# Retention's prompt outputs placed behind its states, sample columns in a segment of their own

## The chip, the cores and the metric

The kernel runs on one core of one Trainium2 chip. The metric is the device time of one execution in microseconds (us). Before the change the median of three runs is 2833.42 us (2832.51 to 2833.78). A change of about 0.2% is what such a measurement can tell from none.

## The reference

One decoder layer is computed for two groups of tokens that share all weights: a prompt of 256 tokens with 16 learned tokens ahead of it, and 8 single sample tokens that continue from given recurrent states.

```python
x <- LN1(alpha*x + 0.5*SwiGLU_1(x))
x <- LN2(alpha*x + Mixer(x))
x <- LN3(alpha*x + 0.5*SwiGLU_2(x))
```

The mixer projects x (2048 features) to ten parts of 2048 and runs two recurrences side by side: retention (8 heads of 256 x 256 state, a fixed decay gamma per head) and HGRN2 (16 heads of 128 x 128 state, a data-dependent decay per feature). Each is normalised per head, gated, summed and projected back. The part that the change touches is retention:

```python
inner = (q @ k.T) * D                       # D: decay between positions, causal
o     = inner @ v + (q * decay) @ S         # output of a chunk from scores and state
S_new = gamma**C * S + (k * decay).T @ v    # state after the chunk
```

For the prompt, S starts at zero, so all 272 positions can be done with scores alone, and S_new is an output. For each of the 8 sample tokens (C = 1) the given state is updated, S_new = gamma*S + k v, which is an output too; its row of the result is q S_new. Outputs of the program are the new activations of both groups and the four sets of states.

## The kernel before

**Tiling.** Features lie on the 128 partitions, tokens along the free dimension: 280 columns (16 learned, 256 prompt, 8 sample), or 264 where the learned ones are not needed. A weight matrix is streamed in units of eight 128 x 128 blocks (512 KB). For each unit SP issues a load into `raw` (three buffers), ScalarE makes a rounded copy `whi` (L172) and VectorE the remainder `wlo` (L173); both have three buffers. The activations are split in the same way. `dense` (L191) then does three matmuls for each block (L198 to L200): `whi` with the high part, `whi` with the low part, `wlo` with the high part.

**Order.** On TensorE (PE) instructions run in exactly the order in which the program text issues them. On VectorE (DVE), ScalarE (ACT), GpSimd (POOL) and the DMA queues a planner sets the order beforehand: it simulates the engines with its own costs, and at each point gives an engine the ready instruction that comes first in the text (weights are put first). On the chip each engine keeps that order and waits at an instruction whose inputs are late. Tiles with one name or tag share a few buffers, given out in the order of the text; `tmp` (L489) maps some names to rows `d0` to `d15` and others that the first FFN's norm has left free.

**Mixer.** The projections of the mixer are done in eight units (`qkv_groups`, `gate_groups`): for each pair of HGRN2 heads and its retention head, two output chunks each of f, q, i (HGRN2), q, k, v (retention), and one unit later the gates. A group of two chunks is one run of `dense` with 16 turns, two blocks or six matmuls a turn. After each turn `pump` (L532) moves every live *thread* on: `mix_hg` and `mix_ret` are generators, and `yield n` means that the next part is issued n turns later. So the small matmuls of both recurrences lie between the large ones of the projections. `mix_hg` is started 3 turns behind the evacuation of i, 25 turns in the second unit (L580); `mix_ret` 3 turns behind v (L594). The small matmuls take PSUM from four `mx` banks, the projections from four `acc` banks.

**Retention in `mix_ret` (L787).** In order of the text: transposes of v and k with their splits into `vtr` and `ktr` (L794 to L813; the last 16 to 24 rows go to `vtl` and through a row called `sro`); the sample rows of v are written to DRAM (`vrow`, L815); scores `psc` (L820), multiplied with the decay table and split into `sch`, `scl`, `ss3`; states `psr` for both halves of the features (L834 to L844), each copied to `sro` and written out. Then the samples, in two halves of four tokens (L847): `vbr` is loaded, a broadcast of four rows of v to all partitions (512 KB, one buffer); for each half c of the features the states `smr` are loaded (512 KB, three buffers, which `ktr` shares), scaled by gamma on ACT (L855), updated by four DVE instructions (L858) and written out; 12 turns later 16 small matmuls read them (`pqr`, L867) against `qdr`, where each token's q stands in a 32-column slot of its own. The first half's rows are copied to `os` (named `osr` in the profile), the second half's added (L873). `os` is split into `orh` and `orl`. Five turns later follow the outputs `por`, one PSUM bank for each half of the features: columns 0 to 255 from scores and v (L884, L887), columns 256 to 263, the samples, from `orh` and `orl` with a selection matrix (L889), and one copy of all 264 columns to `on` (L890). Head normalisation follows, and then `done_r` marks the unit as ready for its gates (L604).

## Time and profile before

| What | Value |
|---|---|
| Median of the runs | 2833.42 us |
| The profiled execution | 2830.58 us |
| Its span, first to last instruction | 2828.6 us |
| PE busy | 2794.1 us, 99% |
| DVE busy | 1723.7 us, 61% |
| ACT busy | 1370.5 us, 48% |
| DMA | 190 GB/s on average |
| Mixer, from the evacuation of its first group to its last projection | 820 to 1969 us of the span |

All times inside the execution count from the first instruction. The page groups instructions by line, engine, operation and tile (out <- in); a line can be that of a helper. PE is matmuls, PEld weight loads; matmuls overlap in the records, so their ends overlap the next one's start. A wait is the idle time of an engine just before an instruction, put down to what released it. In the views by windows, PEclk is the share of its full clock that TensorE was granted.

### The profile page before, as it was taken

To read this page: it belongs to the slowest core of one execution; us is meant where nothing else is said; L and a number is where in the kernel's file an instruction comes from. 1 tells how busy PE (TensorE), PEld (TensorE's weight loads), DVE (VectorE), ACT (ScalarE), POOL (GpSimd) and SP (SyncE) were. 2 spreads that over 40 slices of the span, in tenths; PEclk is the share of its full clock that TensorE was granted. 3 is DMA by queue.
4 is the path that set the end of the run, shared out by engine and by line. 5 is a ranking of instruction groups with operands and counts; after the bars stand their busy time and mean duration, and the time that the engine had idled before them with its cause. 6 is when DMAs were issued, how large, how long until landed. Compare 5 with 4: busy or idle time off the path is not lost.

```text
span 2828.6 us, 54706 instructions
## 1 busy us (share of the span) xinstructions
PE 2794.1 (99%) x22720; PEld 2759.8 (98%) x22720; DVE 1723.7 (61%) x2821; ACT 1370.5 (48%) x2114; POOL 3.4 (0%) x38
## 2 busy tenths in 40 slices
PE   9999999999999999999999999999999999999999
PEld 9999999999999999999999999999999999999998
DVE  5444444554487777676767776776884444446444
ACT  4444443433354564646565655555554444444333
POOL 0000000000000000000000000000000000000000
PEclk9999999999999999999999999999999999999999
DMA  6555555555557575666665756575555555555654
GB/s 223 172 173 175 174 172 174 172 175 172 174 160 231 175 244 190 216 203 215 198 222 186 240 184 230 180 245 166 180 177 185 184 182 184 183 185 180 180 182 140
DMA packets 155594, 536.29 MB, mean 190 GB/s; under 512 B 17937, under 2 KB 27089, under 8 KB 155345
## 3 DMA queue, kind: packets, MB, share of 16 engines
q1 hardware_dynamic: 155200, 532.65, 59.1%
q8 instruction: 178, 2.92, 0.4%
q14 instruction: 72, 0.58, 0.1%
q10 hardware_dynamic: 144, 0.14, 0.0%
HBM read 502.12 MB, written 30.61 MB: 188 GB/s over the span
## 4 chain that ended last, share of the span: by engine, by line
PE 93%; DVE 2%; DMA 2%; ACT 1%; issue 1%; SPq 0%; ACTq 0%; DVEq 0%
PE up L199 12%; PE up L198 12%; PE up L200 12%; PE dn L199 6%; PE dn L200 6%; PE dn L198 6%; DMA smr<-in_sr 2%; PE pj_v_r L198 1%; PE pj_f L199 1%; PE pj_k_r L198 1%; PE pj_k_r L199 1%; PE pj_v_r L199 1%; PE pj_f L198 1%; PE pj_f L200 1%; PE pj_k_r L200 1%; PE pj_v_r L200 1%
## 5 line engine op out<-in xcount | busy, mean ns | idle before, releaser
L173 DVE TENSOR_TENSOR wlo<-raw,whi 128x1024 fp32r<-128x1024 f32 (+1 forms) x869 | 1062.2, 1222 | 869.3 <-ACT whi L172 862.0
L172 ACT CAST whi<-raw 128x1024 fp32r<-128x1024 f32 (+1 forms) x869 | 909.4, 1046 | 1112.8 <-PE up L199 475.5
L199 PE MATMUL up<-x,whi 128*128 128x280 f32 (+1 forms) x2688 | 773.9, 288 | 0.1
L198 PE MATMUL up<-x,whi 128*128 128x280 f32 (+1 forms) x2688 | 767.5, 286 | 1.1 <-ACT whi L172 1.1
L200 PE MATMUL up<-x,wlo 128*128 128x280 f32 (+1 forms) x2688 | 764.7, 284 | 1.2 <-DVE wlo L173 1.2
L198 PEld LDWEIGHTS up<-x,whi 128*128 128x128 f32 x2688 | 505.8, 188 | 1.9 <-ACT whi L172 1.6
L200 PEld LDWEIGHTS up<-x,wlo 128*128 128x128 f32 x2688 | 505.7, 188 | 1.7 <-DVE wlo L173 1.7
L199 PEld LDWEIGHTS up<-x,whi 128*128 128x128 f32 x2688 | 505.4, 188 | 0.3 <-DVE x L206 0.3
L200 PE MATMUL dn<-h,wlo 128*128 128x280 f32 (+1 forms) x1376 | 395.7, 288 | 0.0
L199 PE MATMUL dn<-h,whi 128*128 128x280 f32 (+1 forms) x1376 | 395.6, 288 | 0.0
L198 PE MATMUL dn<-h,whi 128*128 128x280 f32 (+1 forms) x1376 | 391.9, 285 | 0.0
L198 PEld LDWEIGHTS dn<-h,whi 128*128 128x128 f32 x1376 | 259.1, 188 | 0.1
L199 PEld LDWEIGHTS dn<-h,whi 128*128 128x128 f32 x1376 | 258.4, 188 | 0.1
L200 PEld LDWEIGHTS dn<-h,wlo 128*128 128x128 f32 x1376 | 258.3, 188 | 0.0
L198 PE MATMUL pj_i_h<-x,whi 128*128 128x280 f32 x256 | 75.6, 295 | 6.6 <-DVE q L214 6.2
L198 PE MATMUL pj_g_r<-x,whi 128*128 128x264 f32 x256 | 81.7, 319 | 0.0
L858 DVE SCALAR_TENSOR_TENSOR smr<-vbr,k_r,smr 128x256 f32<-128x256 f32 x128 | 55.2, 479 | 39.1 <-DMA vbr<-vrd 38.2
L199 PE MATMUL pj_i_h<-x,whi 128*128 128x280 f32 x256 | 76.2, 298 | 1.6 <-DVE x L366 1.5
L198 PE MATMUL pj_g_h<-x,whi 128*128 128x264 f32 x256 | 76.0, 297 | 0.0
L200 PE MATMUL pj_i_h<-x,wlo 128*128 128x280 f32 x256 | 75.7, 296 | 0.0
L198 PE MATMUL pj_k_r<-x,whi 128*128 128x280 f32 x256 | 75.1, 293 | 0.0
L198 PE MATMUL pj_v_r<-x,whi 128*128 128x280 f32 x256 | 75.1, 293 | 0.0
(374 smaller groups left out, 5314.2 us busy)
## 6 DMA issues: line engine op xcount, KB each, us to landing
raw<-in_w_up SPq DMA_DIRECT2D x343, 512.0 KB
raw<-in_w_in SPq DMA_DIRECT2D x320, 512.0 KB
raw<-in_w_dn SPq DMA_DIRECT2D x172, 512.0 KB
smr<-in_sr SPq DMA_DIRECT2D x32, 512.0 KB
out_srs<-smr SPq DMA_DIRECT2D x32, 512.0 KB
raw<-in_w_out SPq DMA_DIRECT2D x32, 512.0 KB
smh<-in_sg SPq DMA_DIRECT2D x16, 512.0 KB
out_sgs<-smh SPq DMA_DIRECT2D x16, 512.0 KB
```

Source lines behind the costliest of these rows:

```text
L172: nc.scalar.copy(hi[:, j0:j1, :], raw[:, j0:j1, :])
L173: nc.vector.tensor_tensor(out=lo[:, j0:j1, :], in0=raw[:, j0:j1, :], in1=hi[:, j0:j1, :].bitcast(F32), op=ALU.subtract)
L198: nc.tensor.matmul(o, wh, h, start=k == 0, stop=False)
L199: nc.tensor.matmul(o, wh, l, start=False, stop=False)
L200: nc.tensor.matmul(o, wl, h, start=False, stop=k == nk - 1)
L858: nc.vector.scalar_tensor_tensor(out=sm[:, j, :], in0=vb[:, j, :], scalar=k[:, c, t : t + 1], in1=sm[:, j, :], op0=ALU.mult, op1=ALU.add)
```

## The change

In `mix_ret` the order of the text becomes: transposes; the first half's loads (`vbr` and two `smr`) ahead of the scores; scores; states; then, two turns behind the last state and two turns apart, the two `por` groups with columns 0 to 255 alone and a copy of 256 columns each; two turns later the first half's scaling and updates; 6 turns later its read and copy to `os`, and at once the second half's loads; 10 turns later the second half's updates; 6 turns later its read and the addition; 4 turns later the sample columns, a segment of its own: for each half of the features one plain fp32 matmul of `os` with the selection matrix into a new bank `pos`, and one copy of both to `on`. Head normalisation follows at once. The split of `os` is gone, and with it `orh`, `orl` and the rounded selection matrix `sel_r`.

Two more edits: the small `ktl` gets the name and row `d9`, and `sro`, the copy of the state, alternates between rows `d9` and `d11`; and `mix_hg` starts 8 turns behind i in the first unit instead of 3, and 30 instead of 25 in the second.

```diff
-    sel_r = cst.tile([P, NS], F32R, tag="sel_r", name="sel_r")
...
-    nc.scalar.copy(sel_r, sel)
...
@@ -482,7 +480,7 @@
 
             rows = {n: (r if isinstance(r, list) else [r]) for n, r in {
                 "cos": "d0", "sin": "d1", "gs": ["d2", "d3"], "gt": ["d4", "d5"], "y": "d6", "rot": ["d7", "d8"],
-                "sro": "d9", "osh": "d10", "osr": "d11", "vtl": "d11", "T2": "d12", "T4": "d13", "sqh": "ls1", "sq2": "ls2", "kth": "d14", "hhi": "d14", "hlo": "d15", "pr0": "d14", "pr1": "d15", "pr2": "d10", "rhi": "ls2", "orh": "ls2", "orl": "lnc", "dtab": ["d7", "d8"], "rlo": "lnc",
+                "ktl": "d9", "sro": ["d9", "d11"], "osh": "d10", "osr": "d11", "vtl": "d11", "T2": "d12", "T4": "d13", "sqh": "ls1", "sq2": "ls2", "kth": "d14", "hhi": "d14", "hlo": "d15", "pr0": "d14", "pr1": "d15", "pr2": "d10", "rhi": "ls2", "dtab": ["d7", "d8"], "rlo": "lnc",
                 "sqr": "lnq", "hmean": "lnc", "rv": "rv", "rr": "rr", "rt": "rt",
             }.items()}
 
@@ -577,7 +575,7 @@
                     v = tmp("v", (P, 2, T))
                     nc.scalar.copy(v[:, 0, :], o0)
                     nc.scalar.copy(v[:, 1, :], o1)
-                    start(mix_hg(c0 // 2, st["f"], st["k"], st["q"], v), 25 if c0 == 2 else 3)
+                    start(mix_hg(c0 // 2, st["f"], st["k"], st["q"], v), {0: 8, 2: 30}.get(c0, 3))
                 elif n in ("q_r", "k_r"):
                     sc, w, x0 = (1.0, TL, NMETA) if n == "q_r" else (KSC, T, 0)
                     r = tmp(n, (P, 2, w))
@@ -807,13 +805,42 @@
                         nc.vector.tensor_scalar(out=kh[:, b, c, :], in0=kb, scalar1=d, scalar2=None, op0=ALU.mult)
                         nc.vector.scalar_tensor_tensor(
                             out=kl[:, b, c, :], in0=kb, scalar=d, in1=kh[:, b, c, :].bitcast(F32), op0=ALU.mult, op1=ALU.subtract)
-                    ktl = tmp("sro", (P, P))
+                    ktl = tmp("ktl", (P, P))
                     nc.scalar.activation(ktl[:NB2, :], pt[:NB2, 2 * P : 3 * P], AF.Copy, scale=dec[:NB2, 2, u : u + 1])
                     stack(lambda r: ks3[r, c, :], ktl[:NB2, :], 64)
                     yield 2
                 nc.vector.tensor_copy(qdr[:, :, 0 : NS * 32 : 33], q[:, :, SEQ:])
                 vrow = rows_out(vtl[16:24].rearrange("p c f -> p (c f)"), 256, "vr")
 
+                def load(e):
+                    vb = tmp("vbr", (P, 4, 256))
+                    nc.sync.dma_start(vb, vrow[4 * e : 4 * e + 4, :].partition_broadcast(P))
+                    sms = [tmp("smr", (P, 4, 256), bufs=3) for c in range(2)]
+                    for c, sm in enumerate(sms):
+                        nc.sync.dma_start(sm, A["sr"][u, c, :, 4 * e : 4 * e + 4, :])
+                    return vb, sms
+
+                def update(e, vb, sms):
+                    for c, sm in enumerate(sms):
+                        nc.scalar.mul(sm, sm, GAMMA[u])
+                        for j in range(4):
+                            t = LP + 4 * e + j
+                            nc.vector.scalar_tensor_tensor(
+                                out=sm[:, j, :], in0=vb[:, j, :], scalar=k[:, c, t : t + 1], in1=sm[:, j, :],
+                                op0=ALU.mult, op1=ALU.add)
+                        nc.sync.dma_start(O["srs"][u, c, :, 4 * e : 4 * e + 4, :], sm)
+
+                def read(e, sms):
+                    pq = mx_bank("pqr")
+                    for c in range(2):
+                        for j in range(4):
+                            b = 4 * e + j
+                            nc.tensor.matmul(
+                                pq[32 * j : 32 * j + 32, :256], qdr[:, c, 32 * b : 32 * b + 32], sms[c][:, j, :],
+                                start=c == 0, stop=c == 1, tile_position=(0, 32 * j))
+                    return pq[:, :256]
+
+                first = load(0)
                 psc = mx_bank("psc")
                 for b, (col, l0, n, nk) in enumerate(SCORES):
                     for c in range(2):
@@ -843,38 +870,6 @@
                     nc.sync.dma_start(O["srp"][u, c], so)
                     yield 2
 
-                os = tmp("osr", (P, 256))
-                for e in range(2):
-                    vb = tmp("vbr", (P, 4, 256))
-                    nc.sync.dma_start(vb, vrow[4 * e : 4 * e + 4, :].partition_broadcast(P))
-                    sms = []
-                    for c in range(2):
-                        sm = tmp("smr", (P, 4, 256), bufs=3)
-                        sms.append(sm)
-                        nc.sync.dma_start(sm, A["sr"][u, c, :, 4 * e : 4 * e + 4, :])
-                        nc.scalar.mul(sm, sm, GAMMA[u])
-                        for j in range(4):
-                            t = LP + 4 * e + j
-                            nc.vector.scalar_tensor_tensor(
-                                out=sm[:, j, :], in0=vb[:, j, :], scalar=k[:, c, t : t + 1], in1=sm[:, j, :],
-                                op0=ALU.mult, op1=ALU.add)
-                        nc.sync.dma_start(O["srs"][u, c, :, 4 * e : 4 * e + 4, :], sm)
-                    yield 12
-                    pq = mx_bank("pqr")
-                    for c in range(2):
-                        for j in range(4):
-                            b = 4 * e + j
-                            nc.tensor.matmul(
-                                pq[32 * j : 32 * j + 32, :256], qdr[:, c, 32 * b : 32 * b + 32], sms[c][:, j, :],
-                                start=c == 0, stop=c == 1, tile_position=(0, 32 * j))
-                    if e == 0:
-                        nc.scalar.copy(os, pq[:, :256])
-                    else:
-                        add(os, os, pq[:, :256])
-                hilo = tmp("orh", (P, 256), dt=F32R), tmp("orl", (P, 256), dt=F32R)
-                split(*hilo, os)
-                yield 5
-
                 on = tmp("on_r", (P, 2, TL), bufs=2)
                 on_r[u] = on
                 for c in range(2):
@@ -885,10 +880,22 @@
                                 po[:, l0 : l0 + n], x[:, b, c, :], w[:, col : col + n], start=b + i == 0, stop=False)
                     l0 = SCORES[2][1]
                     nc.tensor.matmul(po[:, l0 : l0 + NMETA], vs3[:, c, :], ss3, start=False, stop=True)
-                    for i, x in enumerate(hilo):
-                        nc.tensor.matmul(po[:, SEQ:TL], x[:, c * P : (c + 1) * P], sel_r, start=i == 0, stop=i == 1)
-                    nc.scalar.copy(on[:, c, :], po[:, :TL])
-                    yield 1
+                    nc.scalar.copy(on[:, c, :SEQ], po[:, :SEQ])
+                    yield 2
+                update(0, *first)
+                yield 6
+                os = tmp("osr", (P, 256))
+                nc.scalar.copy(os, read(0, first[1]))
+                second = load(1)
+                yield 10
+                update(1, *second)
+                yield 6
+                add(os, os, read(1, second[1]))
+                yield 4
+                po = mx_bank("pos")
+                for c in range(2):
+                    nc.tensor.matmul(po[:, c * NS : (c + 1) * NS], os[:, c * P : (c + 1) * P], sel, start=True, stop=True)
+                nc.scalar.copy(on[:, :, SEQ:TL], po[:, : 2 * NS].rearrange("p (c b) -> p c b", c=2))
                 sm_ = tmp("sqr", (P, TL))
                 add(sm_, on[:, 0, :], on[:, 1, :])
                 hilo = tmp("rhi", (P, TL), dt=F32R), tmp("rlo", (P, TL), dt=F32R)
```

## The prediction

> **What bounds the kernel now.** I read the page first, then who TensorE waited for, then the granted clock in windows around those waits, and last the order of single instructions in one unit.

> ```profile
> span 2828.6 us, 54706 instructions
> PE 2794.1 (99%) x22720; PEld 2759.8 (98%) x22720; DVE 1723.7 (61%) x2821; ACT 1370.5 (48%) x2114; POOL 3.4 (0%) x38
> ...
> ```

> TensorE (PE) is the bound. It idles 34.5 us of 2828.6, so any gain must come from that idle time or from time that it spends at a lower clock. The waits of PE name most of the idle time (who waited for whom: total us, times, longest):

> ```profile
> PE por L889 <- ACT orh L205: 8.4, 6, 1.9
> PE pj_i_h L198 <- DVE q L214: 6.2, 1, 6.2
> PE por L889 <- DVE orl L206: 4.6, 6, 0.8
> PE pd L211 <- ACT prodsmh L205: 2.0, 1, 2.0
> ...
> PE pqr L867 <- DVE smr L858: 0.9, 1, 0.9
> PE psr L840 <- DVE vs L529: 0.8, 1, 0.8
> ```

> The two rows on L889 are 13.0 us: in six of eight units the sample matmul inside the retention output waits for the rounded copy `orh` of the sample rows, and then once more for its remainder `orl`. The windows below show a second cost. The first four are the 3.4 us stretches that hold such waits, the others stretches that follow a wait, and the last is ordinary work. After the length come PE busy time and its matmuls; PEclk is the first number after POOL.

> ```profile
> 1172.60:1176.01 3.41, 0.79 (x6) 0.61 (x6) 3.37 (x10) 0.48 (x3) 0.00 (x0) 1.00 0.68 213
> 1612.91:1616.33 3.42, 2.48 (x19) 2.39 (x20) 1.77 (x4) 0.66 (x3) 0.00 (x0) 1.00 0.99 307
> 1752.86:1756.27 3.41, 1.56 (x14) 1.39 (x12) 3.41 (x8) 1.74 (x4) 0.00 (x0) 1.00 0.60 201
> 1899.64:1903.05 3.41, 1.59 (x13) 1.43 (x12) 2.72 (x7) 0.79 (x2) 0.10 (x1) 1.00 0.87 312
> 848.33:851.74 3.41, 3.25 (x14) 3.12 (x14) 3.14 (x10) 0.00 (x0) 0.00 (x0) 0.50 0.31 126
> 920.01:926.84 6.83, 4.17 (x18) 4.17 (x19) 6.80 (x20) 3.96 (x13) 0.00 (x0) 0.50 0.84 285
> 1176.01:1182.83 6.82, 6.82 (x33) 6.82 (x33) 1.11 (x3) 2.71 (x5) 0.00 (x0) 0.50 0.45 139
> 1322.78:1329.61 6.83, 6.83 (x34) 6.83 (x33) 1.23 (x3) 2.89 (x6) 0.00 (x0) 0.50 0.41 121
> 1469.55:1476.38 6.83, 6.83 (x33) 6.83 (x33) 1.11 (x3) 2.71 (x5) 0.00 (x0) 0.50 0.41 138
> 1756.27:1763.10 6.83, 6.29 (x29) 6.30 (x30) 1.95 (x6) 2.45 (x4) 0.00 (x0) 0.50 0.55 180
> 1903.05:1909.87 6.82, 6.82 (x33) 6.82 (x33) 1.69 (x4) 3.80 (x6) 0.00 (x0) 0.50 0.25 84
> 1183.00:1189.83 6.83, 6.83 (x69) 6.49 (x67) 4.35 (x8) 3.73 (x8) 0.00 (x0) 1.00 0.33 98
> ```

> At a granted clock of 0.50, PE does 33 or 34 matmuls in 6.83 us instead of 69, so each such stretch costs half its length, 3.4 us. Five of them (from 1176.01, 1322.78, 1469.55, 1756.27 and 1903.05) begin right behind a stretch with an L889 wait. The stretch at 1612.91, 0.94 us idle, is followed by none; those with 1.82 us idle (1899.64) and more are. So the point from which a wait costs double lies between 0.94 and 1.82 us of idle time in a window of 3.4 us. An L889 wait costs some 2 us of idle time plus 3.4 us of slow clock, and PE still shows as busy in the second part.

> [...]

> **Why L889 waits.** One unit (the third), with PE first, then VectorE (DVE), ScalarE (ACT) and the DMA queue (SP); in brackets the idle time before a row and its releaser:

> ```profile
> 1142.52 0.88 PE L838 MATMUL psr<-vtr,ktr 128*128 128x256 f32 x6
> ...
> 1154.87 1.07 PE L867 MATMUL pqr<-smr,qdr 128*32 128x256 f32 x16
> ...
> 1166.63 1.07 PE L867 MATMUL pqr<-smr,qdr 128*32 128x256 f32 x16
> 1171.35 0.22 PE L750 MATMUL pst<-vm,km 128*128 128x128 f32 x1
> ...
> 1171.82 0.48 PE L884 MATMUL por<-sch,vtr 128*128 128x256 f32 x2
> ...
> 1174.63 0.27 PE L889 MATMUL por<-sel_r,orh 128*128 128x8 f32 x1 [1.86 <-ACT orh L205]
> ```

> ```profile
> 1159.86 0.88 DVE L858 SCALAR_TENSOR_TENSOR smr<-vbr,k_r,smr 128x256 f32<-128x256 f32 x2 [5.63 <-DMA vbr<-vrd]
> ...
> 1164.40 1.67 DVE L858 SCALAR_TENSOR_TENSOR smr<-vbr,k_r,smr 128x256 f32<-128x256 f32 x4
> ...
> 1172.42 1.39 DVE L742 SCALAR_TENSOR_TENSOR smh<-vbh,k,smh 128x128 f32<-128x128 f32 x5
> 1173.73 0.41 DVE L217 TENSOR_TENSOR osr<-osr,pqr 128x256 f32<-128x256 f32 x1
> 1174.06 1.22 DVE L173 TENSOR_TENSOR wlo<-raw,whi 128x1024 fp32r<-128x1024 f32 x1
> 1175.20 0.41 DVE L206 TENSOR_TENSOR orl<-osr,orh 128x256 fp32r<-128x256 f32 x1
> ```

> ```profile
> 1148.59 1.06 ACT L855 ACTIVATE smr<-smr 128x1024 f32<-128x1024 f32 x1 [1.06 <-DMA smr<-in_sr]
> ```

> ```profile
> 1152.41 0.46 SPq L849 DMA_DIRECT2D vbr<-vrd  x1
> ```

> DVE idles 5.63 us for the second broadcast `vbr` (issued at 1152.41, used at 1159.86), is then busy without a break, and reaches the addition of the second half's sample rows only at 1173.73, 6.0 us after `pqr` ended (1166.63 + 1.07). The rounding on ACT, a weight split of 1.22 us and the remainder follow.

> **The change part by part.** A step below is one turn of the projection loop (six matmuls). From the end of the second `pqr` (1167.70) to `pst` (1171.35) are five steps: 0.73 us each.

> *Prompt outputs behind the states, the sample columns alone at the end.* The `por` matmuls move up to 2 and 4 steps behind the last `psr`. Their inputs (scores, `vtr`) are ready there, so no wait goes with them. Both pieces are the same matmuls in another place, 1.1 us each (1171.82 to 1172.8 without the wait): 0. Out go `orh` and `orl`; what comes in is two plain fp32 matmuls of 8 columns on the unrounded rows and one 16-column copy. The nearest fp32 row is the other branch's:

> ```profile
> L774 PE MATMUL po<-sel,osh x32: 175/216/256, 913.2 to 1917.5; 128*128 128x8 f32 x32
> L889 PE MATMUL por<-sel_r,orh x16: 252/273/354, 936.9 to 1903.8; 128*128 128x8 f32 x16
> ```

> It records two for each of its 16 heads, so two matmuls are four records of 0.2 us against four of 0.27 us now: 0, at most 0.2 us a unit either way. ACT and DVE lose 0.4 us a unit each, ACT gains a copy no longer than that; both hide behind PE's 0.73 us steps.

> Does `pos` still wait? Steps from `psr` to the first read go from 14 to 12, with 2.2 us of `por` now in between: read at 1154.87 - 1.5 + 2.2 = 1155.6. Reads go from 12 to 16 steps apart, so the second one stands at 1155.6 + 11.76 (today's distance) + 4 x 0.73 = 1170.3, and `pos`, four steps and `pst` (0.47) on, at 1170.3 + 1.07 + 2.92 + 0.47 = 1174.8. DVE's backlog starts 0.7 us later than today with the first read, so its five `smh` end near 1173.7 + 0.7 = 1174.4 at best, the addition near 1174.8; add 0.45 us from there to PE (1174.14 to 1174.6 for `orh` today): `pos` waits about 0.5 us. Bounds: 0 (the addition is put ahead of the `smh`), and 1.9 (all of DVE's work shifts by the 2.2 us of `por`: 1176.3 + 0.4 against 1174.8). I take 0.6 in six units: 3.6 us lost. Both L889 rows go: 13.0 us gained. At 0.6 us idle, below 0.94, the five slow stretches go too: 5 x 3.4 = 17.1 us gained.

> *Samples loaded ahead, updates listed later.* No transfer is added. The planner already issues well ahead of the text: the L855 of 1148.59 scales a tile whose place in the text is behind the read of 1154.87. So I expect about the same queue orders, and DVE's 5.6 us wait for `vbr` to stay. Behind that wait in DVE's order stand weight splits, and it has been survived by the weights converted ahead. The second read gets 4 steps more: the 0.9 us `pqr` wait goes. `sro` in two buffers takes out ACT's wait for the state write, which has cover anyway: 0.

> ```profile
> ACT sro L842 <- DMA out_srp<-sro: 13.4, 7, 3.4
> ```

> *HGRN2 started 5 steps later in units 0 and 1.* In unit 0 PE waits 2.0 us for `prodsmh`:

> ```profile
> 847.87 0.51 PE L211 MATMUL pd<-prodsmh,ones_r 128*128 128x512 f32 x1 [2.00 <-ACT prodsmh L205]
> ...
> 918.38 1.06 ACT L855 ACTIVATE smr<-smr 128x1024 f32<-128x1024 f32 x1 [3.92 <-DMA smr<-in_sr]
> ...
> 922.67 0.60 PE L198 MATMUL pj_i_h<-x,whi 128*128 128x280 f32 x1 [6.24 <-DVE q L214]
> ```

> Five steps are 3.7 us, more than 2.0, and DVE works off the normalisation in them: 2.0 us and the stretch at 848.33 (3.41 / 2 = 1.7) go, 3.7 us; bounds 0 and 3.7. What is late next in unit 0 is the 6.2 us wait for `q`: ACT stands 3.92 us at the sample load of 918.38, with the evacuation of `q` behind it. That load is still issued behind the first read, so I leave this wait and its slow stretch (920.01, 3.4) where they are; bounds 0 and 9.6 us of gain.

> *Less cover.* DVE and ACT get 5 us less per unit for the same work. DVE is at 61% on the page, and the stretch of slow clock was cover for it. I take 0; bound, by the `psr` row, one wait of 0.8 us a unit: 6 us.

> **Sum.** 13.0 + 17.1 + 0.9 + 3.7 - 3.6 = 31.1 us. The profiled execution took 2830.58 us (span 2828.6 and 2 us around it): 2799.5. The median of the runs is 2.84 us above that execution, so 2802. By the bounds: at best 31.1 + 3.6 + 9.6 = 44.3 less (2789); at worst without new slow stretches 31.1 - 7.5 (rest of the 1.9 us waits) - 3.7 - 6 = 13.9 less (2819). Likeliest range 2793 to 2812.

> **Rivals.**
> *The wait moves to `pos` whole* (18%). DVE's backlog is older than the rounding: the addition itself comes at 1173.73, after PE wanted its result. If it slips by the full 2.2 us, the 8.4 us stay, only the 4.6 go, and two to five slow stretches stay. Gains 4.6 + 0.9 + 3.7 plus 0 to 10.2 us: 2814 to 2824, say 2819. For it: the `smh` row just ahead of the addition. Against it: four steps more between the reads, and no work of ACT and no second wait behind the addition.

> *The `q` wait of unit 0 goes too* (12%): 2802 - 9.6 = 2792, if the later HGRN2 start and the later update move ACT's sample scaling behind the evacuation of `q`. Against: the scaling is ready by the planner's reckoning before `q` ends.

> *The slow stretches stay without the waits* (3%). If the half clock does not come from these waits, only idle time is saved: 2802 + 17.1 = 2819. [...]

> *Slower: the second read waits for the updates* (8%). If ACT and DVE keep to the place in the text, the second half's scaling starts 10 steps behind the first read, near 1165.6; one L855 (1.06), eight L858 (1.67 for four, so 3.3) and two weight splits (2.4) end near 1172.4, 2.1 us after PE wants the read at 1170.3. That is above 1.82, so a slow stretch follows: 5.5 us in each of eight units, 44 us against 34.7 gained: 2843. It decides from about 1 us of waiting on (34.7 / 8 = 4.3 us a unit with the 3.4). Against it: the L855 at 1148.59, which runs ahead of its text.

> *Nothing moves* (7%): the planner's order absorbs the edit, one wait is swapped for others of its size; 2833.

> **How the numbers follow.** My forecast has 52%. From 2789 to 2824 are this case, the `q` case, the moved wait and the stretches that stay: 85%. Within 0.2% (5.7 us, what a measurement of this kernel can tell from no change) is "nothing moves". Faster: 52 + 12 + 18 + 3 = 85%; same 7%; slower 8%.

> **What would show it.** Right: no PE wait for `orh` or `orl`, a wait at the new sample matmul under 0.9 us, no granted clock of 0.50 between 1100 and 1970 us, no wait at `pd`; DVE still idle for `vbr`. Wrong: a wait at `pos` of 1.8 us or more with half clock behind it, a wait at the second sample read, or PE waiting for weights because DVE lost its cover.

## The result and the profile after

The changed kernel takes 2794.25 us in the median of four runs (2792.13 to 2796.78), beside 2832.97 us for the kernel before on the same chip (2829.51 to 2833.78, four runs). The ratio is 0.9866, with a 95% interval from 0.9849 to 0.9883: 38.7 us or 1.3% faster. I had predicted 2802 us, in a range from 2789 to 2824. The profiled execution took 2794.69 us; its span, 2792.6 us, is 36.1 us shorter than the one before.

The page after, its first lines (the span; busy time, share and instructions of each engine):

```profile
span 2792.6 us, 54731 instructions
...
PE 2770.2 (99%) x22720; PEld 2738.7 (98%) x22720; DVE 1723.6 (62%) x2813; ACT 1363.8 (49%) x2111; POOL 3.4 (0%) x38
```

PE has as many matmuls as before, and is busy 23.9 us less (2794.1 - 2770.2): it does the same work faster, for the most part because the clock is higher (0.998 of full speed on average in this execution, 0.991 in the one before; 2.8 us have another source, shown below). Its idle time fell by 12.1 us, from 34.5 to 22.4 (2792.6 - 2770.2). What PE waits for now, in the view of waits (who waited for whom: total us, times, longest):

```profile
PE pst L748 <- DVE km L527: 4.9, 6, 1.2
PE pj_i_h L197 <- DVE q L213: 3.6, 2, 3.2
PE up L197 <- ACT x L204: 2.5, 1, 2.5
PE pj_i_h L198 <- DVE x L365: 1.8, 2, 1.5
```

No row is left for `orh` or `orl`, for `prodsmh` or for the second sample read. Nor is there one for the new sample matmul `pos`. A new row leads instead: in six units the HGRN2 state matmul `pst` waits for `km`, 0.8 us on average. In a second execution of the same kernel that wait is 2.7 us in four units, so its size differs from one execution to the next. (Line numbers of helpers are one lower than before: L197 to L199 are the three matmuls of a block.)

The windows after: 1100 to 1970 us of the span, where the kernel before had five stretches of half clock, and then the one long wait for `q` and the stretch behind it. PEclk is the first number after POOL.

```profile
1100.00:1970.00 870.00, 864.74 (x7331) 845.62 (x7330) 625.73 (x1193) 503.74 (x913) 1.57 (x16) 1.00 0.64 213
914.10:917.51 3.41, 0.86 (x8) 0.66 (x6) 3.41 (x8) 2.57 (x5) 0.00 (x0) 1.00 0.63 202
917.51:924.34 6.83, 5.78 (x24) 5.44 (x25) 3.68 (x10) 2.21 (x8) 0.00 (x0) 0.50 0.97 324
```

Between 1100 and 1970 us PE runs at full clock throughout. The stretch at 917.51 is the only one left inside the mixer in this execution.

The same unit as shown of before (the third), PE and then DVE, in order of time:

```profile
1148.14 1.05 PE L838 MATMUL pqr<-smr,qdr 128*32 128x256 f32 x16
...
1162.58 1.07 PE L838 MATMUL pqr<-smr,qdr 128*32 128x256 f32 x16
...
1166.68 0.30 PE L748 MATMUL pst<-vm,km 128*128 128x128 f32 x1 [0.66 <-DVE km L527]
...
1168.04 0.51 PE L897 MATMUL pos<-sel,osr 128*128 128x8 f32 x4
```

```profile
1145.59 1.22 DVE L172 TENSOR_TENSOR wlo<-raw,whi 128x1024 fp32r<-128x1024 f32 x1
1148.03 1.23 DVE L172 TENSOR_TENSOR wlo<-raw,whi 128x1024 fp32r<-128x1024 f32 x1 [1.22 <-ACT whi L171]
1151.07 1.67 DVE L828 SCALAR_TENSOR_TENSOR smr<-vbr,k_r,smr 128x256 f32<-128x256 f32 x4 [1.82 <-DMA vbr<-vrd]
...
1159.78 0.35 DVE L740 SCALAR_TENSOR_TENSOR smh<-vbh,k,smh 128x128 f32<-128x128 f32 x1
...
1164.66 1.21 DVE L172 TENSOR_TENSOR wlo<-raw,whi 128x1024 fp32r<-128x1024 f32 x1
...
1166.25 0.28 DVE L527 TENSOR_TENSOR km<-ptk,km 16x128 fp32r<-16x128 f32 x1
...
1166.92 0.41 DVE L216 TENSOR_TENSOR osr<-osr,pqr 128x256 f32<-128x256 f32 x1
```

The addition ends at 1167.33, and `pos` starts at 1168.04 without a wait. The last of the `smh` updates now lies at 1159.78, far ahead of the addition; before, five of them stood directly in front of it. What is late is `km`, ready at 1166.53 behind a weight split that begins at 1164.66.

By stages, from the first matmul of a stage to that of the next, in both traces (us):

| Stage | shorter by | my terms for it |
|---|---|---|
| Start and first FFN | -2.5 | 0 |
| First unit, to f of the second (883.68, now 880.99) | 5.2 | 3.7 |
| Second unit, to q_r of the third (1086.79, now 1080.28) | 3.8 | 0.9 |
| Units three to eight, mixer's end, next up projection (to 2560.71, now 2527.45) | 26.8 | 26.5 |
| Last down projection to the end | 2.8 | 0 |
| Sum | 36.1 | 31.1 |

The 26.5 are 13.0 + 17.1 - 3.6; the 0.9 is the wait at the second sample read, which lies in the second unit (at 1023.7 us in the kernel before). The other 2.6 us or so of that unit are the shorter wait for `q`. The first row is the wait of the first up projection for its activations (2.5 us in the row of `up` above), which differs between executions: the first up projection took 528.2 to 531.3 us over all kernels here.

### The profile page after: what moved, and what is told of

It reads as the page before. It is cut to its first block, busy times and chain, and to the rows that moved or that the text cites. A ratio compares the mean times of both kernels' runs of the same rounds, so it can differ in the third digit from the quotient of the medians.

```text
span 2792.6 us, 54731 instructions
## 1 busy us (share of the span) xinstructions
PE 2770.2 (99%) x22720; PEld 2738.7 (98%) x22720; DVE 1723.6 (62%) x2813; ACT 1363.8 (49%) x2111; POOL 3.4 (0%) x38
## 3 DMA queue, kind: packets, MB, share of 16 engines
q8 instruction: 178, 2.92, 0.4%
## 4 chain that ended last, share of the span: by engine, by line
PE 94%; DVE 2%; DMA 2%; ACT 1%; issue 1%; SPq 0%; ACTq 0%; DVEq 0%
PE up L198 12%; PE up L197 12%; PE up L199 12%; PE dn L198 6%; PE dn L197 6%; PE dn L199 6%; PE pj_v_r L197 1%; PE pj_f L198 1%; PE pj_k_r L198 1%; PE pj_v_r L198 1%; PE pj_k_r L197 1%; PE pj_f L199 1%; PE pj_f L197 1%; PE pj_k_r L199 1%; PE pj_v_r L199 1%; PE wo L199 1%
## 5 line engine op out<-in xcount | busy, mean ns | idle before, releaser
L198 PE MATMUL up<-x,whi 128*128 128x280 f32 (+1 forms) x2688 | 774.1, 288 | 0.1
L197 PE MATMUL up<-x,whi 128*128 128x280 f32 (+1 forms) x2688 | 767.5, 286 | 3.8 <-ACT x L204 2.5
L199 PE MATMUL up<-x,wlo 128*128 128x280 f32 (+1 forms) x2688 | 764.8, 285 | 0.8 <-DVE wlo L172 0.7
L197 PEld LDWEIGHTS up<-x,whi 128*128 128x128 f32 x2688 | 505.8, 188 | 4.6 <-ACT x L204 2.8
L199 PEld LDWEIGHTS up<-x,wlo 128*128 128x128 f32 x2688 | 505.9, 188 | 1.2 <-DVE wlo L172 1.2
L198 PEld LDWEIGHTS up<-x,whi 128*128 128x128 f32 x2688 | 505.6, 188 | 0.3 <-DVE x L205 0.3
L198 PE MATMUL dn<-h,whi 128*128 128x280 f32 (+1 forms) x1376 | 395.6, 287 | 0.0
L197 PE MATMUL dn<-h,whi 128*128 128x280 f32 (+1 forms) x1376 | 392.6, 285 | 0.0
L199 PE MATMUL dn<-h,wlo 128*128 128x280 f32 (+1 forms) x1376 | 390.8, 284 | 0.0
L197 PEld LDWEIGHTS dn<-h,whi 128*128 128x128 f32 x1376 | 258.5, 188 | 0.1
L199 PEld LDWEIGHTS dn<-h,wlo 128*128 128x128 f32 x1376 | 258.5, 188 | 0.0
L198 PEld LDWEIGHTS dn<-h,whi 128*128 128x128 f32 x1376 | 258.3, 188 | 0.1
L197 PE MATMUL pj_i_h<-x,whi 128*128 128x280 f32 x256 | 75.2, 294 | 3.9 <-DVE q L213 3.6
L197 PE MATMUL pj_g_r<-x,whi 128*128 128x264 f32 x256 | 79.0, 309 | 0.0
L198 PE MATMUL pj_i_h<-x,whi 128*128 128x280 f32 x256 | 75.5, 295 | 1.9 <-DVE x L365 1.8
L197 PE MATMUL pj_g_h<-x,whi 128*128 128x264 f32 x256 | 75.5, 295 | 0.0
L197 PE MATMUL pj_v_r<-x,whi 128*128 128x280 f32 x256 | 75.0, 293 | 0.0
L197 PE MATMUL pj_k_r<-x,whi 128*128 128x280 f32 x256 | 74.9, 293 | 0.0
L199 PE MATMUL pj_i_h<-x,wlo 128*128 128x280 f32 x256 | 74.9, 293 | 0.0
L198 PE MATMUL pj_v_r<-x,whi 128*128 128x280 f32 x256 | 74.5, 291 | 0.0
```

The lines of the kernel that those rows point to most:

```text
L197: nc.tensor.matmul(o, wh, h, start=k == 0, stop=False)
L198: nc.tensor.matmul(o, wh, l, start=False, stop=False)
L199: nc.tensor.matmul(o, wl, h, start=False, stop=k == nk - 1)
```

## The experiments

Every kernel below computes the whole reference. Times are medians, with the range where there are several runs; a time without a range is a single run; ratios are to the kernel before on the same chip.

**Is it the rounding or the addition that is late?** The kernel before without `orh` and `orl`, everything in its old place:

```diff
-                hilo = tmp("orh", (P, 256), dt=F32R), tmp("orl", (P, 256), dt=F32R)
-                split(*hilo, os)
                 yield 5
...
-                    for i, x in enumerate(hilo):
-                        nc.tensor.matmul(po[:, SEQ:TL], x[:, c * P : (c + 1) * P], sel_r, start=i == 0, stop=i == 1)
+                    nc.tensor.matmul(po[:, SEQ:TL], os[:, c * P : (c + 1) * P], sel, start=True, stop=True)
```

> The kernel before with the rounding of the sample rows alone taken out: columns 256 to 263 come from the unrounded rows in plain fp32, at the same place in the text, five turns behind the second read. Theory A (the addition itself is late, at 1173.73 in the third unit where the matmul is wanted at 1172.77): a wait remains, now for the addition, of about 1.4 us instead of 1.9 + 0.8 in that unit (1174.14 + 0.05 against 1172.77) and 0.3 to 1.4 us in the other five; most stretches at half clock go, since the wait is below 1.8 us; 13.0 - 5 + 5 x 3.4 is up to 25 us gained, with some stretches left 12 to 20. Theory B (the rounding chain on ScalarE and VectorE is the whole cause): no wait at the sample matmul at all, 30 us gained.

Measured: 2815.33 us (2808.07 to 2817.34), ratio 0.9933 (0.9916 to 0.9950). The waits of PE:

```profile
PE por L886 <- DVE osr L217: 5.7, 6, 1.5
```

With neither rounding nor remainder, PE still waits in the same six units, now for the addition itself: 5.7 us of the 13.0. So the addition is late by itself, and the split adds 7.3 us. In the profiled execution one stretch of half clock stays among these six units. It begins at 1460.25 us, behind a wait that leaves 1.45 us idle in its window (3.41 less PE's 1.96):

```profile
1456.84:1460.25 3.41, 1.96 (x19) 1.87 (x17) 3.38 (x10) 0.60 (x3) 0.00 (x0) 1.00 0.67 207
1460.25:1463.66 3.41, 3.41 (x18) 3.41 (x17) 0.98 (x3) 1.96 (x3) 0.00 (x0) 0.50 0.93 294
```

The other five waits leave at most 1.25 us in a window, and no stretch follows them. This execution is the fastest of the four (2808.07 us, mean granted clock 0.997); the other three have 0.995, so they hold more half clock than the trace shows. By the median it is 17.6 us of the gain, without moving anything.

**Is distance alone enough?** The kernel before, with four more turns between the split and the outputs:

```diff
                 split(*hilo, os)
-                yield 5
+                yield 9
```

> The kernel before with nine turns instead of five between the split of the sample rows and the outputs; nothing else. Rival: all that was missing is distance, and the new order of the text is not needed. Four turns are 2.9 us, the waits were at most 1.9 + 0.8: then no wait for orh or orl, no half clock behind the outputs, about 27 to 30 us gained, the 2 us wait of the first unit and its slow stretch left. If the planner fills the time with other work ahead of the addition instead, waits of 1 us or more stay and the gain is under 20 us.

Measured: 2804.64 us (2802.92 to 2807.77), ratio 0.9901 (0.9885 to 0.9918). Waits of PE, and one window row for the same 870 us:

```profile
PE pj_i_h L198 <- DVE q L214: 6.1, 1, 6.1
PE pd L211 <- ACT prodsmh L205: 2.0, 1, 2.0
```

```profile
1100.00:1970.00 870.00, 868.28 (x7355) 848.54 (x7355) 628.10 (x1192) 505.57 (x909) 1.59 (x16) 1.00 0.66 214
```

One number changed gives 28.3 us of the 38.7 (2832.94 - 2804.64): no wait for `orh` or `orl` is left, and these units run at full clock. So most of what the change brings comes from this, that the sample columns come later than their inputs, not that the prompt outputs come earlier. Here `pst` does not wait for `km` either.

**And if the distance is taken back?** The changed kernel with one turn instead of four between the addition and `pos`:

```diff
                 add(os, os, read(1, second[1]))
-                yield 4
+                yield 1
```

> The changed kernel with one turn instead of four between the second read and the sample matmul. The addition of the rows comes 3.3 us behind the end of the second read in the third unit (1163.6 to 1166.9), and the sample matmul is wanted 2.2 us earlier than now: it should wait 2 to 2.5 us there, and 1 to 2.5 us in the units behind. If idle time of 1.8 us or more in a 3.4 us window brings half clock (the threshold read from the trace of before), three or more of these units get a stretch at 0.50 of 3.4 or 6.8 us, and the profiled time rises by 10 to 25 us. If half clock has nothing to do with such waits, only the idle time is added: 6 to 12 us.

Measured: 2821.15 us. The waits, and two pairs of windows (the second pair is the wait of 3.34 us at 1453.78 with what follows it; the first pair holds one of 2.64 us that ends at 1165.70):

```profile
PE pos L897 <- DVE osr L216: 17.4, 6, 3.3
```

```profile
1161.16:1164.57 3.41, 1.90 (x22) 1.11 (x22) 3.38 (x5) 1.91 (x5) 0.00 (x0) 1.00 0.86 350
1164.58:1167.99 3.41, 2.29 (x19) 2.29 (x20) 1.90 (x5) 0.79 (x3) 0.00 (x0) 1.00 0.87 291
1451.30:1454.71 3.41, 0.93 (x8) 0.93 (x8) 2.44 (x6) 0.17 (x1) 0.00 (x0) 1.00 0.74 240
1454.71:1458.12 3.41, 3.41 (x18) 3.41 (x17) 1.15 (x3) 1.60 (x3) 0.00 (x0) 0.50 0.37 148
```

Three turns less cost 27 us against the changed kernel, a little more than the 10 to 25 I expected, since the waits are longer (2.4 to 3.3 us): 17.4 us of waits and four stretches of half clock. The rest of the change is in place here, so without these turns it brings little. The `km` wait is gone here (PE stands at `pos` instead), and one thing I had not expected shows: the wait of 2.64 us is longer than any single L889 wait of before (1.9 us), and no half clock follows it. It lies across a border: 1.51 us of idle time in one window and 1.12 in the next. The borders are counted in steps of 3.41 us from the start of the stretch at 1454.71 (1164.58 lies 85 steps ahead of it); that starts of such stretches lie whole steps apart is read from the trace of before, further down. With 2.48 us idle in one such window half clock follows here, with 1.51 and 1.12 us in two it does not.

**The later HGRN2 start.** The changed kernel with the old start turns, and with `sel_r` left among the constants:

```diff
-                    start(mix_hg(c0 // 2, st["f"], st["k"], st["q"], v), {0: 8, 2: 30}.get(c0, 3))
+                    start(mix_hg(c0 // 2, st["f"], st["k"], st["q"], v), 25 if c0 == 2 else 3)
```

> The changed kernel with HGRN2 started 3 and 25 turns behind i in the first two units, as before, and the unused rounded selection matrix kept, so that all tiles lie as before. The 2.0 us wait at pd comes back, with 1.7 us of half clock: 3.7 us slower than the changed kernel; later units unchanged. If the last down projection takes 251 us again and not 248, its 2.8 us come from where the tiles lie; if 248, from the execution.

Measured: 2799.02 us (2795.46 to 2803.12), ratio 0.9881 (0.9865 to 0.9896).

```profile
PE pst L750 <- DVE km L529: 4.3, 6, 1.2
PE pj_i_h L198 <- DVE q L214: 3.8, 2, 2.8
...
PE pd L211 <- ACT prodsmh L205: 2.0, 1, 2.0
```

The 2.0 us wait at `pd` is back, so the start is what removes it. The 1.7 us of half clock that I expected with it are not: the wait leaves 1.83 us idle in its window, and the next one runs at full clock.

```profile
846.54:849.96 3.42, 1.58 (x14) 1.37 (x12) 3.30 (x8) 1.71 (x3) 0.00 (x0) 1.00 0.48 155
849.96:853.37 3.41, 3.09 (x21) 2.73 (x22) 3.30 (x9) 0.88 (x3) 0.00 (x0) 1.00 0.49 154
```

The `q` wait is 3.8 us as in the changed kernel (3.6), so the start is not what shortened that. The `km` wait is not its work either. Of the 4.8 us to the changed kernel's time, 2.8 belong to `sel_r`, as a later experiment shows; the other 2.0 fit the wait, but are within the spread of the runs.

**The updates' place and the buffer of `sro`.** Two edits of the changed kernel: the second half's updates directly behind their loads; and `sro` back in one buffer.

```diff
                 second = load(1)
-                yield 10
                 update(1, *second)
-                yield 6
+                yield 16
```

> The changed kernel with the second half's updates listed right behind its loads, and 16 turns from there to the read. Theory A (the planner runs ahead of the text, the place of the updates hardly matters): the time of the changed kernel within 3 us, VectorE's wait for the second broadcast stays near 17 us in total. Rival: listing the updates later is what shortened that wait from 38 to 17 us and cleared VectorE; then it goes back towards 38 us, waits come back behind the second read and the time rises by 10 us or more.

```diff
-"sro": ["d9", "d11"]
+"sro": "d9"
```

> The changed kernel with one buffer for the copy of the state instead of two. If ScalarE's wait for the state write (13.4 us before) had no part in the gain, the time is that of the changed kernel within 3 us and VectorE's wait for the second broadcast stays near 17 us. If the second buffer is what let VectorE's wait shrink from 38 us, it goes back above 30 us, and TensorE's wait for km grows.

Measured: 2799.31 us (2791.86 to 2803.65) and 2792.22 us. DVE's waits for the broadcast `vbr`, of the first and of the second kernel:

```profile
DVE smr L828 <- DMA vbr<-vrd: 14.0, 9, 4.2
```

```profile
DVE smr L828 <- DMA vbr<-vrd: 11.8, 7, 5.4
```

And the same wait before, and after the change:

```profile
DVE smr L858 <- DMA vbr<-vrd: 38.2, 8, 6.4
```

```profile
DVE smr L828 <- DMA vbr<-vrd: 16.7, 7, 5.6
```

Neither edit brings the 38.2 us back. The differences below 17 us say little: a second execution of the changed kernel has 11.3. With one buffer, ACT waits 16.2 us for the state's write again, and the time is that of the changed kernel: no gain from the second buffer shows here. With the early updates the time is 5.1 us above that of the changed kernel where I expected at most 3, but the ratios overlap (0.9879, 0.9859 to 0.9898, against 0.9866, 0.9849 to 0.9883), so this is not clear of noise. Its trace has 7.4 us of `km` wait, with a stretch of half clock at 1732.50; two executions of the changed kernel have 4.9 and 2.7. Why it is longer is not shown.

**The loads ahead of the scores.** Taken out of the change, and put into the kernel before by themselves:

```diff
-                first = load(0)
                 psc = mx_bank("psc")
...
+                first = load(0)
                 update(0, *first)
```

> The changed kernel with the first half's sample loads directly ahead of its updates in the text, instead of ahead of the scores; nothing else moved. DVE's wait for the second broadcast fell from 38.2 us (8) to 16.7 us (7) with the change. Theory A: it fell because the first half is loaded ahead; here it is over 30 us again. Theory B: it fell because the prompt outputs stand ahead of the samples, so that more weight splits lie between the two halves; here it stays under 20 us. The time hardly moves by either (2792 to 2800), unless the late update makes a wait of 1.8 us or more at the first read or at the state of HGRN2.

```diff
+                first = load(0)
                 psc = mx_bank("psc")
...
                 for e in range(2):
-                    vb = tmp("vbr", (P, 4, 256))
-                    nc.sync.dma_start(vb, vrow[4 * e : 4 * e + 4, :].partition_broadcast(P))
-                    sms = []
+                    vb, sms = first if e == 0 else load(1)
```

> The kernel before with the first half's sample loads ahead of the scores in the text, as the change has them; prompt outputs, split and all else as before. Theory A (the loads ahead shorten the wait for the second broadcast): DVE's wait for it under 20 us instead of 38, the wait for the rounded sample rows shorter by 1 to 2 us in each unit, fewer stretches of half clock: 2805 to 2825. Theory B (the loads do nothing by themselves): 38 us stays, the waits for the rounded rows stay at 13 us, and the time is within 5 us of 2833.

Measured: 2789.19 and 2831.80 us, beside 2831.01 us for the kernel before. First the changed kernel without them, then the kernel before with them:

```profile
DVE smr L828 <- DMA vbr<-vrd: 10.9, 9, 3.7
```

```profile
DVE smr L862 <- DMA vbr<-vrd: 39.9, 9, 6.2
```

My theory that the early loads shortened the wait for `vbr` falls both ways, and they bring no time: the kernel before with them alone is where it was, the changed kernel without them is no slower. The waits of PE for `orh` and `orl` are all there in the second of them, 9.2 and 4.6 us. What differs after the change is the place of weight splits in DVE's order. They fill more of the gap, as the DVE rows of the third unit show: two in the last 5.5 us ahead of the first use of the broadcast, while before the last one began 6.9 us ahead of it, at 1153.00. Part is the broadcast itself: from its issue to its first use pass 7.45 us before (1152.41 to 1159.86) and 6.32 after (1144.75 to 1151.07). This is read from one unit; no run separates the two. What makes the planner choose that order was not separated: the prompt outputs ahead of the samples and the 16 turns between the two reads (12 before) are what remains.

**Where do 2.8 us in the last down projection come from?** Nothing of the change touches that stage. But `sel_r` is gone from the constants, 32 bytes in each partition, and every tile behind it lies 32 bytes lower. The kernel before, with `sel_r` moved to the mixer's own memory and nothing else:

```diff
-    sel_r = cst.tile([P, NS], F32R, tag="sel_r", name="sel_r")
...
+            sel_r = mp.tile([P, NS], F32R, tag="sel_r", name="sel_r")
+            nc.scalar.copy(sel_r, sel)
```

> The kernel before with the rounded selection matrix (32 bytes a partition) taken out of the constants and put into the mixer's own pool, so that tiles allocated behind the constants lie 32 bytes lower, as in the changed kernel. Layout theory: the last down projection takes 248.0 us instead of 250.8, everything else stays, 2.8 us gained. Otherwise it takes 250.8 again and the 2.8 us belong to something else in the change.

Measured: 2823.49 us. The last down projection's third matmul by form (matmuls; busy us, mean ns of one) and 240 us of that stage, before, then after, and last the same 240 us in this kernel:

```profile
L200 PE MATMUL dn<-h,wlo 128*128 128x264 f32 x688 | 196.2, 285 | 0.0
...
2565.00:2805.00 240.00, 240.00 (x1978) 239.93 (x1977) 128.37 (x158) 91.95 (x99) 0.00 (x0) 1.00 0.58 178
```

```profile
L199 PE MATMUL dn<-h,wlo 128*128 128x264 f32 x688 | 191.3, 278 | 0.0
...
2530.00:2770.00 240.00, 240.00 (x2001) 239.93 (x2000) 129.19 (x159) 93.50 (x102) 0.00 (x0) 1.00 0.56 178
```

```profile
2558.00:2798.00 240.00, 240.00 (x2000) 239.93 (x2000) 129.75 (x160) 94.44 (x102) 0.00 (x0) 1.00 0.58 179
```

At full clock and without a wait, PE does 1978 matmuls in 240 us with `sel_r` in the constants (121.3 ns each) and 2000 or 2001 without (119.9 ns). From its first matmul to the last, the stage takes 250.85 us in the kernels traced with it there (the kernel before, and those without the split, with more turns, with the old HGRN2 start and with the loads put into the kernel before), and 248.02 us in those without. So 2.83 us of the gain come from where tiles lie, and not from the retention's order. Why 32 bytes matter is not shown. The waits for `orh` and `orl` are all there in this kernel, 10.4 and 4.6 us, with four stretches of half clock in these units instead of five. The two stretches of the first unit, at 834.67 and 848.33 before, are missing in this execution too. Beyond the 2.83 us, its time lies under the 2833.82 us of the kernel before on its chip (2823.97 to 2839.52) by chance of this kind.

**Can the rest of the `q` wait be had?** First with two edits together: the changed kernel with the first unit's retention 12 turns behind v instead of 3, and HGRN2's two sample blocks 9 and 11 turns apart.

```diff
-start(mix_ret(c0 // 2, st["q_r"], st["k_r"], v), 3)
+start(mix_ret(c0 // 2, st["q_r"], st["k_r"], v), 12 if c0 == 0 else 3)
...
                     nc.sync.dma_start(O["sgs"][2 * u + h], sm)
-                    yield 9
+                    yield 9 + 2 * h
```

> A try at a faster one: the changed kernel with the first unit's retention started 12 turns behind v instead of 3, and for the second head of each HGRN2 unit 11 turns instead of 9 between the transposes of K and the state. The first takes ScalarE's wait for the last sample load out from ahead of the evacuation of q in the first unit: 3.6 us of idle time and some 3 us of half clock. The second gives the late km 1.5 us, more than its longest wait of 1.2: 4.9 us. Together up to 11 us under the changed kernel, near 2783; if the waits only move on to the next matmul of the branch, the time stays within 3 us of 2794.

Then the first edit alone, and beside it the changed kernel as it is:

> The changed kernel itself once more, beside the next one on the same chip. Expected by every theory: its earlier 2794 us within 4, and the stretch of half clock behind the 3.2 us wait for q in the first unit again.

> The changed kernel with retention of the first unit started 12 turns behind v instead of 3, and nothing else moved. An earlier run that also spread HGRN2's samples had no half clock behind q and gained 3.4 us in the first two units, but lost 6.5 us in the units behind them. Theory A: the loss came from the spread samples alone; this kernel keeps units 2 to 7 as they are in the changed kernel and is 3 to 6 us faster than it: 2788 to 2791. Theory B: the later retention pushes every later unit's ACT and DVE work, and the loss stays: 2797 to 2800.

Measured: 2798.53 us (2796.05 to 2802.32), ratio 0.9879 (0.9849 to 0.9908) with both edits; 2793.57 us (2791.78 to 2793.80), ratio 0.9867 (0.9847 to 0.9888) with the first alone; 2791.85 us (2791.23 to 2792.78), ratio 0.9863 (0.9846 to 0.9881) for the changed kernel itself. The first expectation misses: with both edits the time is no better than the changed kernel's. Waits of PE with both edits, and with the first alone:

```profile
PE pvr L210 <- ACT rhi L204: 5.1, 6, 0.8
PE pos L897 <- DVE osr L216: 4.0, 6, 1.0
```

```profile
PE pst L748 <- DVE km L527: 6.2, 6, 1.3
...
PE pj_i_h L197 <- DVE q L213: 2.0, 2, 1.3
```

Both expectations for the first edit alone miss: it neither gains 3 us nor loses 5. The `q` wait falls to 2.0 us (with both edits too), but `pst` now waits 1.3 us for `km` in the second unit, and by that unit's end the trace is 1.3 us ahead of the changed kernel's. In the traces the units from the third on take 6.4 us longer with both edits than with the first alone (from q_r of the third unit to the next up projection 956.8 and 950.4 us). That goes with the spread samples: only with them do waits appear behind the addition, in six units 0.8 us for `rhi` and up to 1.0 us for `osr`. Their sum, 9.1 us, stands against 4.9 for `km` in the same units. The times themselves do not show a loss: the ratios overlap.

One comparison of windows is worth more than these times. The `q` wait in the kernel with late loads (first row), with the late retention (second and third):

```profile
914.64:918.05 3.41, 1.69 (x16) 1.48 (x12) 3.41 (x8) 2.40 (x5) 0.00 (x0) 1.00 0.67 221
918.05:921.46 3.41, 1.83 (x13) 1.61 (x14) 2.18 (x4) 0.33 (x2) 0.00 (x0) 1.00 1.00 282
```

```profile
912.74:916.15 3.41, 1.52 (x10) 1.30 (x11) 2.08 (x4) 1.18 (x2) 0.00 (x0) 1.00 1.05 284
916.15:919.57 3.42, 3.42 (x23) 2.93 (x25) 1.58 (x4) 0.97 (x3) 0.00 (x0) 0.50 1.03 407
```

The first kernel is idle for 3.3 us in two pieces, 1.72 us in one window and 1.58 in the next (3.41 less PE's busy time), and keeps its clock. The second is idle for 2.0 us, 1.89 of them in one window, and loses it. So here the wait that a border splits is the longer one and yet costs less. A sharp point, though, does not come out of these records. The 1.45 us in the kernel without the split brought half clock, the 1.83 us in the kernel with the old HGRN2 start did not (both shown above). Taking all windows at full clock in the fourteen traces, from 30 us of the span on: none with less than 1.45 us of idle time is followed by half clock, all with 1.85 us or more are, and of the 21 between, 14 are and 7 are not. What else decides there is not shown; the records model the ends of matmuls, so the idle time of a window is itself not exact.

## Why the prediction was right, and where not

**The waits on L889: right.** The step said that both rows, 13.0 us, go, and they went. The kernel with the longer distance shows that distance alone does it.

**The half clock: right.** Five stretches of 3.4 us were to go with the waits, and none is left between 1100 and 1970 us. The rival by which they stay is out. How much idle time was enough: 1.89 us in one window of the kernel with the late retention, shown above. Where the windows lie can be read from the trace of the kernel before: the stretches at 848.33, 920.01, 1176.01, 1322.78, 1469.55, 1756.27 and 1903.05 begin 4, 25, 100, 143, 186, 270 and 313 steps of 3.4133 us behind the one at 834.67, each a whole number, whatever the waits between them. Windows laid in such steps tell the two cases apart: those 1.89 us in one had a stretch behind them, the wait of 2.64 us across a border (1.51 and 1.12) had none.

**The wait at `pos`: size off, and place.** I took 0.6 us in six units, with a bound of 0 if the addition is put ahead of the `smh`. It was that bound. On the clock of before (add 6.55 us, the lead at the unit's projection to v) the second read came at 1169.1 (I had 1170.3), the addition at 1173.5 (I had 1174.4 at the earliest) and `pos` at 1174.6 (I had 1174.8). But a wait of 0.8 us on average appeared one step earlier, at `pst`. In the third unit PE, with `por` now ahead of it, comes to `pst` 1.2 us later (1171.35, now 1173.2 less the wait of 0.66), while `km` comes 2.5 us later on DVE (1170.35, now 1172.8) and had been ready only 0.7 us ahead. I had followed DVE's order to the addition only, and not asked of each product in it who wants it, and when. The two errors cancel nearly, which is luck: 4.9 us lost in this execution (2.7 in the second) instead of 3.6.

**DVE's wait for `vbr`: wrong.** I said it stays, because the planner issues ahead of the text anyway. That is true of the loads, as the two kernels with them moved show. It fell all the same, from 38.2 to 16.7 us; in the third unit weight splits stand in the gap that were not there before. Which part of the change brought that order is open. In the sum it had no term, since no wait of PE was put down to it.

**The first unit: the wait right, its half clock chance.** The wait at `pd`, 2.0 us, went and came back with the old start. The stretch behind it, 1.7 of my 3.7 us, did not come back: of the six traces here that have this wait, only that of the kernel before has the stretch. In four of the others a border splits the wait, and in the kernel with the old start 1.83 us in one window are without effect. The 1.5 us above my term are of the same kind. They belong to a stretch of 1.7 us at 834.67 in the kernel before that I had not listed. Its wait of 1.8 us for `x` is still there after the change, and split by a border of the windows in the profiled execution; in a second execution of the same kernel the stretch is back, at 836.48. So both parts, some 3.4 us between the two profiled executions, are chance and not the change. These are the two executions of the changed kernel:

```profile
832.17:835.59 3.42, 2.21 (x14) 1.54 (x12) 3.42 (x7) 2.00 (x3) 0.00 (x0) 1.00 0.56 180
835.59:839.00 3.41, 2.42 (x17) 2.21 (x17) 3.41 (x10) 0.59 (x2) 0.00 (x0) 1.00 0.51 161
```

```profile
833.07:836.48 3.41, 1.60 (x10) 1.17 (x9) 3.41 (x8) 1.42 (x3) 0.00 (x0) 1.00 0.52 160
836.48:839.89 3.41, 3.41 (x17) 3.41 (x16) 3.41 (x10) 1.23 (x3) 0.00 (x0) 0.50 0.42 153
```

**The `q` wait: size off.** I left it at 6.2 us with 9.6 us as the most that could be had. It fell to 3.6 us and kept its stretch: the rival's mechanism in part. Which piece of the change did it is not settled: with the old HGRN2 start it is 3.8 us, with the late loads 3.3, with the early updates 2.6, and the changed kernel itself has 3.6 in one execution and 2.8 in another. In the five traces without the moved outputs it is 4.7 to 6.2.

**Less cover: the 0 held.** DVE stands at 62%, and no wait for weights appears inside the units.

**Not foreseen:** the 2.8 us in the last down projection. The 5.0 us between my sum (31.1) and the span's 36.1 are these 2.8, 1.5 in the first unit, 2.9 in the second and 0.3 in the six units behind, less 2.5 lost at the start.

**The lower bound: a slip.** Six waits of 1.9 us are 7.8 us above the 3.6 in the sum, not 7.5. And by the rows that the prediction shows, waits of 1.9 us would have kept their slow stretches, so 2819 us was not the worst case.

## What to carry to other kernels

In these traces a wait on TensorE cost its length, and another 1.7 to 3.4 us (half of a stretch of 3.41 or 6.83 us at 0.50) if it left enough idle time in one window of 3.41 us (from 1.85 us on always, from 1.45 us on sometimes); so waits that were cut below that, or split in two by a border, were worth more than their length says. Before a piece is moved, look for the turn count that separates it from its inputs: here one number, 5 to 9 turns, gave 28 of the 39 us. And when work is moved on an engine with an order of its own, go through every product that lies behind it there and ask when its reader wants it: here the wait came up at `pst` (4.9 us for `km`), one reader ahead of the one I had followed. A stretch of half clock behind a wait of about 2 us may be missing in the next execution, as the one at 836.48 is in one of two executions of the changed kernel, so such a gain is counted only when a second trace has it.

## What the runs showed of the hardware

The pace of TensorE in the last down projection went with where tiles lie in a partition: 121.3 ns a matmul with the 32 bytes of `sel_r` ahead of them, 119.9 ns without, at full clock in both, 2.83 us over the stage. The first down projection, with its 280 columns, shows no such difference between the kernels before and after: means of 287, 291 and 290 ns for its three matmuls in both. The cause stays open.
